# A unit's seventh product issued behind the first product of the next unit

## The chip, the cores and the metric

The kernel runs on one core of one Trainium2 chip, as one program with one launch. The metric is the device time of that program in microseconds (us). Five engines matter here: TensorE (PE, matrix products, with PEld for its weight loads), VectorE (DVE), ScalarE (ACT), GpSimd (POOL, which here issues accumulating transfers) and SyncE (SP, which issues the other transfers). Each engine runs its own instructions in a fixed order and waits on semaphores for the others.

## What is computed

The reference is a trunk of two layers over 528 rows (16 learned meta tokens and 512 tokens) of width 1024, in float32. Layer 0 mixes by retention, layer 1 by gated linear attention (GLA), and each layer has a half-step SwiGLU feed-forward part ahead of its mixer and one behind it:

```python
def swiglu(x, w_in, w_out):
    gate, up = jnp.split(x @ w_in, 2, axis=-1)      # 1024 -> 2 * 2816
    return (jax.nn.silu(gate) * up) @ w_out         # 2816 -> 1024

for i in range(DEPTH):                              # DEPTH = 2
    h = h + 0.5 * swiglu(rmsnorm(h, norm_ffn1[i]), ffn1_w_in[i], ffn1_w_out[i])
    hn = rmsnorm(h, norm_mix[i])
    h = h + (retention(hn, ...) if i % 2 == 0 else gla(hn, ...))
    h = h + 0.5 * swiglu(rmsnorm(h, norm_ffn2[i]), ffn2_w_in[i], ffn2_w_out[i])
return rmsnorm(h, final_norm)[:, N_META:]
```

Retention projects q, k, v and a gate g for four heads, rotates q and k, takes decayed scores in chunks, normalises per head, multiplies by silu(g) and projects back.

## The kernel before

**Precision.** Every float32 operand is held as two float32r parts, `hi` and `lo = x - hi`. One product of a 128-row block is therefore three matmuls (`mm3`, lines 473 to 475): hi by hi, hi weights by lo data, lo weights by hi data. A weight tile is split on arrival: ACT casts it to `whi` (line 167), DVE subtracts to get `wlo` (line 168).

**Units.** Most weight matrices are not multiplied tile by tile. Two output tiles of 128 rows, the two halves of the inner dimension and the two halves of the tokens make a 2 x 2 block product, which a *unit* does with seven products in place of eight (Winograd's form). `unit_steps` (line 667) issues them in the order `W.UNIT`: a11, s1, s2, a12, s3, s4, a22. Each is 12 matmuls of 264 columns in the feed-forward input and the retention, and 12 or 9 in the feed-forward output, by how many hidden tiles the group has (256 columns in the last feed-forward part). The letters a and s name the weights: a block of the matrix as it is, or a sum of blocks. s1 and s3 come from a `pair` tile, which SP loads (line 130) and POOL completes with an accumulating transfer (line 136); s2 and s4 are made by DVE in place (lines 173 and 175).

**Accumulators.** A unit has one PSUM bank X, out of a ring of four, and a tile QZ of two banks, out of two such tiles. The products a11, s2, s3 and a22 each need X, one after the other; s1, a12 and s4 go to QZ. So X has to be read out between any two of its products:

- after a11, ACT copies X away (line 695); then s2 may start, with s1 in between
- after s2, ACT copies X (line 699); then s3 may start, with a12 in between
- after s3, `c22` on DVE reads X (line 944 in a gate unit, 968 in an up unit, 1005 in an output unit); then a22 may start, with s4 in between
- after s4, `row1` reads QZ; after a22, `c21` reads X

**What is a unit where.** A feed-forward part (`ffn`, four of them: f10, f20, f11, f21) runs through groups of hidden tiles. For two hidden tiles at a time there is a gate unit g (`unit_g`, its `c21` is a Silu on ACT, line 948) and an up unit u (`unit_u`), after which `hidden` makes the seven combinations of the two hidden tiles and splits them (lines 642 to 644, and 506 and 507). Once a group is whole, its four output units o (`unit_o`) follow the next group's first g, ahead of that group's first u; the last group's follow its last u. Output units add to the residual `x`. In the retention, heads 1 to 3 have units for q, k, two for v and two for the gate; head 0 has units for its gate alone.

**What sets the order.** The code calls the steps in program order. A scheduler then lays the instructions out on each engine by priority; reads of accumulators are issued under `urgent()`, which puts them ahead. The weights follow a plan: `plan_ffn`, `plan_ret` and `plan_gla` list every product in the order of its use (`W.plan`), `get` takes the next entry and insists that it is the one asked for, and `fetch` (called by `hook` after each product) splits the entries ahead, into seven `whi`/`wlo` buffers. Raw loads (seven buffers) and pair loads (three) are begun as earlier ones are split.

Of the kernel before, what the change touches and what calls it, by code (L numbers as in the profile page):

```python
# [16 lines left out]
P = 128  # L17
# [52 lines left out]
class Weights:  # L70
# [10 lines left out]
    def __init__(self, tc, ctx, raw_bufs=7, pair_bufs=3, bufs=7):  # L81
        self.nc, self.tc = tc.nc, tc

        self.behind = None
        self.raw_pool = ctx.enter_context(tc.tile_pool(name="wraw", bufs=raw_bufs))
        self.pair_pool = ctx.enter_context(tc.tile_pool(name="wpair", bufs=pair_bufs))
        self.pool = ctx.enter_context(tc.tile_pool(name="wsplit", bufs=bufs))

        self.homes = [(self.pool, bufs, set())]
        self.ahead = AHEAD  # L90


        self.loads = {"raw": [], "pair": []}
        self.begun = dict.fromkeys(self.loads, 0)
        self.over = dict.fromkeys(self.loads, 0)
        self.room = {"raw": raw_bufs, "pair": pair_bufs}
        self.tiles, self.plan, self.parts = {}, [], {}
        self.split = self.taken = self.keys = 0

    def add(self, key, ap):  # L100
        c = self.keys
        self.keys += 1
        for o in range(0, ap.shape[1], PW):
            part = ap[:, o:o + PW]
            self.loads["raw"].append(((c, o), len(self.plan), (part,)))
            self.plan.append((key, c, o, part.shape[1], None))

    def add_unit(self, key, ap1, ap2, order, parted=False):
        c = self.keys
        self.keys += 1  # L110
        n = ap1.shape[1] // 2
        a = {"a11": ap1[:, :n], "a12": ap1[:, n:], "a21": ap2[:, :n], "a22": ap2[:, n:]}
        self.loads["pair"].append((c, len(self.plan), (a["a11"], a["a22"], a["a21"]), parted))
        for q in ("a11", "a12", "a22"):
            self.loads["raw"].append(((c, q), len(self.plan), (a[q],)))
        for q in order:
            self.plan.append((key + (q,), c, q, n, order))

# [70 lines left out]
    def get(self, key):  # L189

        i = self.taken
# [7 lines left out]
        return [(j,) + self.parts.pop(j) for j in range(i, i + n)]  # L199

# [39 lines left out]
def trunk(ctx, tc, a):  # L240
# [60 lines left out]
    def plan_ret():  # L301
        for h in range(RH):
            for j in (2 * h, 8 + 2 * h):
                if h:
                    W.add_unit(("rqk", j), a["ret_in"][j], a["ret_in"][j + 1], W.UNIT)
# [5 lines left out]
            for s, o in (("rv", 16), ("rg", 32)):  # L311
                for m in range(0, 4, 2):
# [4 lines left out]
                    else:  # L317
                        W.add_unit((s, h, m), a["ret_in"][c], a["ret_in"][c + 1], W.UNIT)
# [348 lines left out]
    def unit_steps(key, name, order, halves, ks, rhs, places, row1, c22, c21, behind=None):  # L667
# [8 lines left out]
        def step(q):  # L676
# [14 lines left out]
            with urgent():  # L691
# [12 lines left out]
                elif q == "a22":  # L704
                    c21(X)

# [8 lines left out]
    def unit(key, name, order, halves, ks, rhs, place, row1, c22, c21, behind=None):  # L715
# [40 lines left out]
    def ffn(which, layer, halves, gcol, u, feed, late=False):  # L756
# [7 lines left out]
        with tc.tile_pool(name=f"h_{me}", bufs=1) as hp, tc.tile_pool(name=f"t_{me}", bufs=1) as tp, \  # L764
# [189 lines left out]
            def unit_u(f, g, first):  # L954
# [16 lines left out]
                def c21(c):  # L971
                    V.scalar_tensor_tensor(y[0][:, 0], c, -1.0, g[1][:, a0:a1], ALU.mult, ALU.mult)
# [44 lines left out]
            for n, (kind, a_, b_) in enumerate(steps):  # L1017
# [39 lines left out]
                else:  # L1057
                    hs = [H[a_][f] for f in sorted(H[a_])]
# [3 lines left out]
                    break  # L1062

# [139 lines left out]
    def retention(u, feed):  # L1203
        with tc.tile_pool(name="retp", bufs=1) as rp, tc.tile_pool(name="wmore", bufs=2) as wp, psum_pool(4) as pp:
# [48 lines left out]
            def head(h):  # L1253
                qk = {}

                def rope_pair(s):
# [15 lines left out]
                    unit(("rqk", j), f"rqk{s}{h}", W.UNIT, HALVES, rows4_odd, rhs_u, place, row1, c22, c21)  # L1272
                    cos, sin = [tabs[s][:, c, :] for c in range(2)]
                    pa, pb = [tmp.tile([P, T], F32, tag="hf", name=f"r{i}{s}{h}") for i in "ab"]
                    V.tensor_mul(pa, t[0], cos)
                    V.tensor_mul(t[0], t[0], sin)
                    V.tensor_mul(pb, t[1], sin)
                    V.tensor_add(pa, pa, pb)
                    qk[s, 0], qk[s, 1] = [[rp.tile([P, T], F32R, tag=f"{s}{i}{m}", name=f"{s}{i}{m}_{h}")
                                           for i in range(2)] for m in range(2)]  # L1280
                    S.copy(qk[s, 0][0], pa)
                    V.tensor_mul(t[1], t[1], cos)
                    V.tensor_sub(t[0], t[0], t[1])
                    V.tensor_sub(qk[s, 0][1], pa, qk[s, 0][0].bitcast(F32))
                    split(qk[s, 1][0], qk[s, 1][1], t[0])
# [35 lines left out]
                def values():  # L1321
# [18 lines left out]
                    for m0 in (0, 2):  # L1340
# [11 lines left out]
                        unit(("rv", h, m0), f"rv{h}{m0}", W.UNIT, HALVES, rows4_odd, rhs_u, place, row1, c22, c21)  # L1352
# [64 lines left out]
                def gates(m0, use):  # L1417
# [19 lines left out]
                    unit(("rg", h, m0), f"rg{h}{m0}", W.UNIT, HALVES, rows4_odd, rhs_u, place, row1, c22, c21)  # L1437
# [785 lines left out]
```

## Time and profile before

| | |
|---|---|
| median of 3 runs | 2050.59 us (2050.23 to 2054.59) |
| profiled execution, its own time | 2055.57 us |
| its span, first to last instruction | 2053.8 us |
| PE busy in the span | 2026.1 us |
| DVE, ACT, POOL busy | 1794.8, 1198.9, 210.3 us |
| mean granted TensorE clock | 0.995 |

A profiled row has its start in us from the span's start, its duration, engine, line, operation, `out<-in` by the program's names without their numbers, and, in brackets, how long the engine stood idle before it and what ended that. A matmul is shown as about 0.28 us long while the next one starts 0.117 us later, since they are pipelined and their ends are modelled. So a gap between two matmuls shows as idle time only from about 0.16 us on, and the share of busy time hides shorter ones: where PE is looked at closely, starts are compared, not idle times.

### The profile page before, as it was taken

How to read it: one execution, taken by the hardware profiler on the slowest of the kernel's cores; microseconds unless marked ns; L12 is line 12 of the kernel's file. 1: busy time of each engine (PE TensorE's matmuls, PEld its weight loads, DVE VectorE, ACT ScalarE, POOL GpSimd, SP SyncE). 2: the span in 40 equal slices, each digit the busy share in tenths (PEclk: the TensorE clock that was granted, in tenths of full speed). 3: DMA queues.
4: the chain of work that ended last, by engine and by line, in shares of the span. 5: the costliest groups of instructions: out<-in, count | busy, mean ns of one | idle time of the engine just before them, and what ended most of it. 6: DMA issues, size and time to landing. Idle time of an engine off the chain costs nothing.

```text
span 2053.8 us, 43086 instructions
## 1 busy us (share of the span) xinstructions
PE 2026.1 (99%) x16335; PEld 1968.4 (96%) x16335; DVE 1794.8 (87%) x3299; ACT 1198.9 (58%) x2435; POOL 210.3 (10%) x181
## 2 busy tenths in 40 slices
PE   8999999999999999999999999999999999999998
PEld 8999999999999999999999999999899988999998
DVE  8988989968787889988898998989897968999996
ACT  5656666554545465656666665666645445666664
POOL 1011111000101000111111011111001000111110
PEclk9999999999999999999999999999999999999999
DMA  7676776445555532776876477676614351687762
GB/s 209 154 196 169 187 191 173 125 131 145 141 143 141 142 105 69 198 192 150 204 184 167 112 187 191 164 196 170 194 53 127 85 165 62 157 218 175 192 176 72
DMA packets 176112, 318.85 MB, mean 155 GB/s; under 512 B 17568, under 2 KB 40736, under 8 KB 175904
## 3 DMA queue, kind: packets, MB, share of 16 engines
q1 hardware_dynamic: 133856, 237.04, 34.8%
q0 software_dynamic: 40896, 75.51, 23.4%
q10 hardware_dynamic: 1152, 3.55, 0.6%
q8 instruction: 128, 2.10, 0.4%
q14 instruction: 80, 0.66, 0.1%
HBM read 311.76 MB, written 4.26 MB: 154 GB/s over the span
## 4 chain that ended last, share of the span: by engine, by line
PE 75%; DVE 16%; ACT 3%; issue 3%; DMA 2%; POOL 0%; SPq 0%; POOLq 0%; DVEq 0%; ACTq 0%
DVE wlo L168 5%; PE po_r L474 1%; PE po_r L475 1%; PE po_r L473 1%; ACT whi L167 1%; DVE hf L507 1%; PE Xf21o L473 1%; PE lv L1753 1%; PE Xf20o L473 1%; PE Xf20o L474 1%; PE Xf20o L475 1%; DVE unf L799 1%; PE Xf21o L475 1%; PE Xf21o L474 1%; PE Xf11u L473 1%
## 5 line engine op out<-in xcount | busy, mean ns | idle before, releaser
L167 ACT CAST whi<-raw 128x512 fp32r<-128x512 f32 (+1 forms) x893 | 525.3, 606 | 453.3 <-DVE raw L173 101.5
L168 DVE TENSOR_TENSOR wlo<-raw,whi 128x512 fp32r<-128x512 f32 (+1 forms) x893 | 586.0, 669 | 135.9 <-ACT whi L167 121.4
L167 ACT CAST whi<-pair 128x512 fp32r<-128x512 f32 (+1 forms) x304 | 183.9, 605 | 95.2 <-ACT su L695 12.8
L168 DVE TENSOR_TENSOR wlo<-pair,whi 128x512 fp32r<-128x512 f32 (+1 forms) x304 | 202.0, 664 | 5.5 <-ACT whi L167 5.4
L136 POOL DMA_DIRECT2D pair<-in_f_in x73 | 89.0, 1220 | 721.7 <-DVE wlo L168 247.8
L173 DVE TENSOR_TENSOR raw<-pair,raw 128x512 f32<-128x512 f32 (+1 forms) x146 | 97.3, 667 | 2.6
L175 DVE TENSOR_TENSOR raw<-raw,raw 128x512 f32<-128x512 f32 (+1 forms) x146 | 97.3, 666 | 2.5
L136 POOL DMA_DIRECT2D pair<-in_f_out x44 | 53.5, 1216 | 367.1 <-DVE wlo L168 118.0
L474 PE MATMUL po_r<-ogl,whi 128*128 128x264 f32 x256 | 71.3, 279 | 0.0
L473 PE MATMUL po_r<-ogh,whi 128*128 128x264 f32 x256 | 71.2, 278 | 0.0
L475 PE MATMUL po_r<-ogh,wlo 128*128 128x264 f32 x256 | 71.2, 278 | 0.0
L136 POOL DMA_DIRECT2D pair<-in_ret_in x20 | 24.4, 1222 | 298.7 <-DVE wlo L168 96.5
L473 PE MATMUL Xf20o<-hf,whi 128*128 128x264 f32 x176 | 50.3, 286 | 0.8 <-DVE x L1005 0.3
L473 PE MATMUL Xf10o<-hf,whi 128*128 128x264 f32 x176 | 50.3, 286 | 0.7 <-DVE x L1005 0.3
L473 PE MATMUL Xf11o<-hf,whi 128*128 128x264 f32 x176 | 50.2, 285 | 0.7 <-ACT hf L506 0.3
L474 PE MATMUL Xf10o<-hf,whi 128*128 128x264 f32 x176 | 49.2, 279 | 0.0
L474 PE MATMUL Xf20o<-hf,whi 128*128 128x264 f32 x176 | 49.1, 279 | 0.0
L474 PE MATMUL Xf11o<-hf,whi 128*128 128x264 f32 x176 | 49.1, 279 | 0.0
L475 PE MATMUL Xf10o<-hf,wlo 128*128 128x264 f32 x176 | 48.9, 279 | 0.0
L475 PE MATMUL Xf20o<-hf,wlo 128*128 128x264 f32 x176 | 48.9, 279 | 0.0
L475 PE MATMUL Xf11o<-hf,wlo 128*128 128x264 f32 x176 | 48.9, 279 | 0.0
L474 PEld LDWEIGHTS po_r<-ogl,whi 128*128 128x128 f32 x256 | 48.0, 188 | 0.0
(1172 smaller groups left out, 8520.1 us busy)
## 6 DMA issues: line engine op xcount, KB each, us to landing
raw<-in_f_in SPq DMA_DIRECT2D x277, 256.0 KB, 4.3
pair<-in_f_in SPq DMA_DIRECT2D x150, 256.0 KB, 4.4
pair<-in_f_in POOLq DMA_DIRECT2D x73, 512.0 KB, 6.9
raw<-in_f_out SPq DMA_DIRECT2D x80, 256.0 KB, 3.7
raw<-in_ret_in SPq DMA_DIRECT2D x76, 256.0 KB, 3.5
raw<-in_f_out SPq DMA_DIRECT2D x72, 192.0 KB, 3.2
pair<-in_f_out SPq DMA_DIRECT2D x48, 256.0 KB, 3.9
pair<-in_f_out POOLq DMA_DIRECT2D x24, 512.0 KB, 6.1
```

Source lines behind the costliest of these rows:

```text
L136: nc.gpsimd.dma_start(t, aps[2].unsqueeze(1).broadcast_to([P, 2, n]), accum_op=ALU.add)
L167: self.nc.scalar.copy(hi[:, :n], raw)
L168: V.tensor_sub(lo[:, :n], raw, hi[:, :n].bitcast(F32))
L173: V.tensor_add(s2, self.tiles[c][:, 1], self.tiles[c, "a11"])
L175: V.tensor_add(raw, raw, s2)
L473: nc.tensor.matmul(ps, lhsT=lh, rhs=rh, start=start, stop=False, **kw)
L474: nc.tensor.matmul(ps, lhsT=lh, rhs=rl, start=False, stop=False, **kw)
L475: return nc.tensor.matmul(ps, lhsT=ll, rhs=rh, start=False, stop=stop, **kw)
L507: V.tensor_sub(lo, src, hi.bitcast(F32))
L799: V.scalar_tensor_tensor(t[:, i, 1 - h, a0:], x[k][:, a0:], ngains[:, gcol + k:gcol + k + 1], rb[:, a0:], ALU.mult, ALU.mult)
L1753: nc.tensor.matmul(ps[:, j, J * P:J * P + n], lhsT=Kt[:, j, J * P:(J + 1) * P], rhs=q, start=(J == 0), stop=(J == 3), skip_group_check=True)
```

## The change

The last product of a unit, a22, is no longer issued as the unit's seventh. `unit` holds it back (`W.held`), the next unit issues its first product, and when that unit asks for its second, the plan has the held a22 first: `get` sees that the entry is not the one asked for and calls `settle`, which issues a22 with all that follows from it (`c21`, and what is now in `done`: `hidden` for an up unit, the rotation for q and k). The plan is written in the same order: `add_unit(..., hold=True)` takes a22 out and puts it behind the next unit's first product (`_planned`), or ahead of whatever else comes next in the plan. The order of loads, splits and frees follows the plan. Nothing else is computed, and no instruction is added or taken away.

Not held are: the up unit of the last two hidden tiles in the three feed-forward parts that are not the last one, the second v unit and the second gate unit of a retention head, and all GLA units. Where no unit follows (after a retention head's k, at the end of a feed-forward part) `settle` issues the held product where it stood before. Of the program's 150 units, 126 have their a22 behind the next one's first product: 27 gate units before an up unit, 9 gate units before an output unit, 35 up units before a gate unit, 36 output units before an output unit, 9 output units before an up unit, and 10 units in the retention.

```diff
@@ Weights
+        self.kept, self.held = [], None
...
     def add(self, key, ap):
+        self._planned()
...
+    def _planned(self):
+        self.plan += self.kept
+        self.kept = []
+
-    def add_unit(self, key, ap1, ap2, order, parted=False):
+    def add_unit(self, key, ap1, ap2, order, parted=False, hold=False):
...
         for q in order:
             self.plan.append((key + (q,), c, q, n, order))
+            self._planned()
+        if hold:
+            self.kept.append(self.plan.pop())
...
     def get(self, key):
+        if self.plan[self.taken][0] != key:
+            self.settle()
...
+    def settle(self):
+        held, self.held = self.held, None
+        if held:
+            held()
@@ plan_ffn, plan_ret
-                           last and b_ == LAST_GROUPS[1][0])
+                           last and b_ == LAST_GROUPS[1][0], last or (a_, b_) != ("u", NF - 2))
...
-                    W.add_unit(key, w_out[layer, b_, :, c], w_out[layer, b_ + 1, :, c], W.UNIT, last and a_ == 0)
+                    W.add_unit(key, w_out[layer, b_, :, c], w_out[layer, b_ + 1, :, c], W.UNIT, last and a_ == 0, True)
...
-                    W.add_unit(("rqk", j), a["ret_in"][j], a["ret_in"][j + 1], W.UNIT)
+                    W.add_unit(("rqk", j), a["ret_in"][j], a["ret_in"][j + 1], W.UNIT, hold=True)
...
-                        W.add_unit((s, h, m), a["ret_in"][c], a["ret_in"][c + 1], W.UNIT)
+                        W.add_unit((s, h, m), a["ret_in"][c], a["ret_in"][c + 1], W.UNIT, hold=m == 0)
@@ unit_steps, unit
                 elif q == "a22":
                     c21(X)
+            if q == "a22" and done:
+                done()
...
-        for st in unit_steps(key, name, order, halves, ks, rhs, places, row1, c22, c21, behind):
+        *steps, last = unit_steps(key, name, order, halves, ks, rhs, places, row1, c22, c21, behind, done)
+        for st in steps:
             st()
+        if hold:
+            W.held = last
+        else:
+            last()
@@ ffn, unit_u
+                def done():
+                    if f < NPL:
+                        todo.append((f, y[0]))
+                    elif not last:
+                        hidden(f, y[0])
+
                 unit((which, layer, "i", "u", f), f"{me}u{f}", W.FIRST if first else W.UNIT, halves, rows4, rhs_in,
-                     place_of[0], row1, c22, c21)
-                if f < NPL:
-                    todo.append((f, y[0]))
-                elif not last:
-                    hidden(f, y[0])
+                     place_of[0], row1, c22, c21, None, done, not last)
...
+            W.settle()
```

Three places show what moves. The first is PE where up unit 18 of the first feed-forward part (f10) follows gate unit 18: the first and last matmul of each product from the gate unit's s4 on, before and now (`Xf10g18` is the gate unit's bank X, `Xf10u18` the up unit's, `QZ` the two-bank tiles).

```order
L475 MATMUL QZf10g18_3844<-uhf10_153,wlo175_3880 128x264
L473 MATMUL Xf10g18_3843<-thf10_231,whi176_3898 128x264
...
L475 MATMUL Xf10g18_3843<-thf10_231,wlo176_3899 128x264
L473 MATMUL Xf10u18_3978<-uhf10_153,whi177_3917 128x264
...
L475 MATMUL Xf10u18_3978<-uhf10_153,wlo177_3918 128x264
L473 MATMUL QZf10u18_3979<-thf10_231,whi178_3934 128x264
...
L475 MATMUL QZf10u18_3979<-thf10_231,wlo178_3935 128x264
L473 MATMUL Xf10u18_3978<-thf10_231,whi179_3952 128x264
```

And in the changed program:

```order
L494 MATMUL QZf10g18_3812<-uhf10_153,wlo175_3880 128x264
L492 MATMUL Xf10u18_3958<-uhf10_153,whi176_3898 128x264
...
L494 MATMUL Xf10u18_3958<-uhf10_153,wlo176_3899 128x264
L492 MATMUL Xf10g18_3811<-thf10_231,whi177_3916 128x264
...
L494 MATMUL Xf10g18_3811<-thf10_231,wlo177_3917 128x264
L492 MATMUL QZf10u18_3959<-thf10_231,whi178_3934 128x264
...
L494 MATMUL QZf10u18_3959<-thf10_231,wlo178_3935 128x264
L492 MATMUL Xf10u18_3958<-thf10_231,whi179_3952 128x264
```

The gate unit's a22 and the up unit's a11 have changed places. Between s3 and a22 of the gate unit now stand two products (s4 and the other unit's a11) where there was one, and between a11 and s2 of the up unit also two (the other unit's a22 and s1).

The second place is ACT over the same stretch: the gate unit's Silu steps (`gf`), the copies out of the up unit's X and QZ, and the weight casts among them. Before:

```order
L940 ACTIVATE gf1018_3841<-gf1018_3841 128x528
L948 ACTIVATE gf1019_3842<-Xf10g18_3843 128x264
L167 CAST whi182_4014<-raw86_3690 128x512
L167 CAST whi183_4033<-raw87_3733 128x512
L167 CAST whi184_4052<-raw88_3752 128x512
L695 COPY su3_3980<-Xf10u18_3978 128x264
L167 CAST whi185_4069<-pair34_3712 128x512
L693 COPY su3_3980<-QZf10u18_3979 128x264
L167 CAST whi186_4088<-raw88_3752 128x512
L699 COPY su3_3980<-Xf10u18_3978 128x264
```

Now:

```order
L966 ACTIVATE gf1018_3809<-gf1018_3809 128x528
L714 COPY su3_3960<-Xf10u18_3958 128x264
L178 CAST whi182_4014<-raw86_3693 128x512
L178 CAST whi183_4033<-raw88_3770 128x512
L178 CAST whi184_4051<-raw87_3733 128x512
L974 ACTIVATE gf1019_3810<-Xf10g18_3811 128x264
L178 CAST whi185_4069<-pair34_3712 128x512
L712 COPY su3_3960<-QZf10u18_3959 128x264
L178 CAST whi186_4088<-raw88_3770 128x512
L718 COPY su3_3960<-Xf10u18_3958 128x264
```

The copy that frees the up unit's X after a11 (L695, now L714) has moved ahead of three weight casts, and the gate unit's `c21` (L948, now L974) behind them.

The third place is ACT after that up unit, where gate unit 20 begins: the casts of `hidden` (`hf1018`) and the copies out of the gate unit's X and QZ. Before:

```order
L506 CAST hf1018_4114<-su3_4073 128x3x264
L695 COPY su3_4130<-Xf10g20_4128 128x264
L506 CAST hf1018_4114<-t0f10h18_4115 128x2x264
L167 CAST whi191_4202<-raw91_3902 128x512
L693 COPY su3_4130<-QZf10g20_4129 128x264
L167 CAST whi192_4219<-pair35_3862 128x512
L506 CAST hf1018_4114<-t1f10h18_4116 128x2x264
L699 COPY su3_4130<-Xf10g20_4128 128x264
```

Now:

```order
L714 COPY su3_4098<-Xf10g20_4096 128x264
L178 CAST whi191_4201<-raw90_3883 128x512
L525 CAST hf1018_4140<-t0f10h18_4141 128x2x264
L525 CAST hf1018_4140<-su3_4073 128x3x264
L712 COPY su3_4098<-QZf10g20_4097 128x264
L178 CAST whi192_4219<-pair35_3850 128x512
L525 CAST hf1018_4140<-t1f10h18_4142 128x2x264
L718 COPY su3_4098<-Xf10g20_4096 128x264
```

The copy after a11 is now ahead of all casts of `hidden`; the copy after s2 (L699, now L718) still stands behind the last of them, and these now belong to a product that PE does one product later than before.

More of the change, by code (lines that the diff above doesn't have):

```diff
@@ L665, in trunk, with unit_steps @@
     ends = {}
-    def unit_steps(key, name, order, halves, ks, rhs, places, row1, c22, c21, behind=None):
+    def unit_steps(key, name, order, halves, ks, rhs, places, row1, c22, c21, behind=None, done=None):
         started, hold = set(), {}
@@ L713, in rows4_odd, with unit @@
         return range(4) if what[0] == "n" and what != "n3" else ODD
-    def unit(key, name, order, halves, ks, rhs, place, row1, c22, c21, behind=None):
+    def unit(key, name, order, halves, ks, rhs, place, row1, c22, c21, behind=None, done=None, hold=True):
         wd = width(halves)
@@ L1350, in c21 @@
                             S.copy(vt[m0 + 1][:, a0:a1], c)
[L1352 removed]
+                        unit(("rv", h, m0), f"rv{h}{m0}", W.UNIT, HALVES, rows4_odd, rhs_u, place, row1, c22, c21,
+                             hold=m0 == 0)
                 def turn(j):
@@ L1435, in c21 @@
                         use(m0 + 1, a0, a1, o)
-                    unit(("rg", h, m0), f"rg{h}{m0}", W.UNIT, HALVES, rows4_odd, rhs_u, place, row1, c22, c21)
+                    unit(("rg", h, m0), f"rg{h}{m0}", W.UNIT, HALVES, rows4_odd, rhs_u, place, row1, c22, c21, hold=m0 == 0)
                     sgs.extend(mine)
```

30 lines of the change are left out of this document (16 added, 14 removed).

## The prediction

> **What bounds the kernel.** The page comes first: busy shares and the chain that ended last.
>
> ```profile
> PE 2026.1 (99%) x16335; PEld 1968.4 (96%) x16335; DVE 1794.8 (87%) x3299; ACT 1198.9 (58%) x2435; POOL 210.3 (10%) x181
> PE 75%; DVE 16%; ACT 3%; issue 3%; DMA 2%; POOL 0%; SPq 0%; POOLq 0%; DVEq 0%; ACTq 0%
> ```
>
> PE is the bound: busy for 99%, and three quarters of the chain. Its idle time, 2053.8 - 2026.1 = 27.7 us, looks like all that a new order could win, and most of it lies outside the units. But a matmul counts as busy for 0.28 us while the next starts 0.117 us later, so short gaps are hidden in the 99%. I therefore measure stretches against the pitch: the view of busy time by stretches, cut at the starts of units. The columns are the stretch, its length, then busy time and instructions of PE, PEld, DVE, ACT and POOL, the granted clock, DMA share and GB/s.
>
> ```profile
> 61.93:113.12 51.19, 50.56 (x422) 49.78 (x421) 50.23 (x89) 34.38 (x70) 6.10 (x5) 1.00 0.71 175
> 113.12:152.32 39.20, 39.20 (x338) 39.20 (x337) 34.31 (x58) 21.77 (x43) 4.87 (x4) 1.00 0.74 192
> 152.32:212.61 60.29, 60.08 (x506) 59.34 (x505) 53.36 (x95) 37.51 (x77) 7.30 (x6) 1.00 0.67 162
> 212.61:243.62 31.01, 31.01 (x255) 30.54 (x254) 27.68 (x55) 19.03 (x42) 4.04 (x4) 1.00 0.77 202
> 243.62:314.19 70.57, 70.23 (x590) 69.25 (x589) 62.27 (x108) 43.73 (x89) 9.35 (x8) 1.00 0.77 194
> 314.19:355.90 41.71, 40.98 (x338) 40.08 (x337) 40.85 (x79) 28.66 (x61) 3.65 (x3) 1.00 0.62 155
> 819.18:1112.61 293.43, 291.65 (x2438) 288.05 (x2437) 266.40 (x475) 183.45 (x376) 35.30 (x29) 1.00 0.72 182
> 1163.22:1456.48 293.26, 291.51 (x2437) 287.64 (x2436) 266.03 (x471) 183.10 (x373) 36.36 (x30) 1.00 0.74 186
> 1812.93:1871.48 58.55, 58.49 (x507) 57.70 (x505) 54.80 (x98) 37.45 (x77) 8.46 (x7) 1.00 0.78 187
> 1871.48:1901.77 30.29, 30.29 (x254) 29.52 (x253) 27.27 (x55) 18.88 (x42) 3.61 (x3) 1.00 0.77 207
> ```
>
> The second row is four output units without any wait: 9.80 us for the 84 matmuls of each (a row's count takes in two or so that overlap its edges), 1.40 us for a product of 12. The first six rows are the first feed-forward part. It has 5 g and u units (49.0 us without waits, 51.19 taken), these 4 o units, 6 g and u (58.8, 60.29), 4 o with 9 matmuls in a product (29.4, 31.01), 7 g and u (68.6, 70.57), 4 o (39.2, 41.71). The excess is 2.2 + 0 + 1.5 + 1.6 + 2.0 + 2.5 = 9.8 us. The second and third parts hold the same 30 units from their second one on (284.2 us): 9.2 and 9.1 us of excess. In the last part a product of 12 should take 1.36 us (256 columns in place of 264, and the pitch in proportion); six g and u units would need 57.1 (58.55 taken), four o units 28.6 (30.29), and three such rounds give about 9. Together **37 us of waits inside units**, though PE shows up as full.
>
> **What the change takes away.** Where do they lie? I go through a gate unit and its up unit by starts: the stretch of each, then the gate unit's a22 on PE and DVE.
>
> ```profile
> 273.71:283.73 10.02, 10.02 (x87) 9.90 (x86) 9.93 (x18) 6.51 (x13) 1.22 (x1) 1.00 0.73 179
> 283.73:293.98 10.25, 10.15 (x87) 9.95 (x86) 8.12 (x15) 6.33 (x13) 1.21 (x1) 1.00 0.75 188
> 281.99 0.28 PE L475 MATMUL QZf10g<-uhf,wlo 128*128 128x264 f32 x1
> 282.19 0.39 PE L473 MATMUL Xf10g<-thf,whi 128*128 128x264 f32 x1
> 282.42 0.28 PE L474 MATMUL Xf10g<-tlf,whi 128*128 128x264 f32 x1
> 281.71 0.42 DVE L944 TENSOR_TENSOR gf<-Xf10g,su 128x264 f32<-128x264 f32 x1
> ```
>
> a22 starts 0.20 us behind the last matmul of s4, not 0.117, and 0.06 us after `c22` on DVE (281.71 + 0.42 = 282.13) has read X; its second matmul comes 0.23 us later, not 0.117. That is 0.08 + 0.11 us, and the unit's whole excess is 10.02 - 9.80 = 0.22 us. In the new order the up unit's a11 stands ahead of it: 1.40 us where some 0.1 lacked, so the wait goes. Next the up unit's s2, on PE and ACT:
>
> ```profile
> 286.41 0.28 PE L475 MATMUL QZf10u<-thf,wlo 128*128 128x264 f32 x1
> 286.79 0.39 PE L473 MATMUL Xf10u<-thf,whi 128*128 128x264 f32 x1
> 283.98 0.65 ACT L940 ACTIVATE gf<-gf 128x528 f32<-128x528 f32 x1 [1.39 <-DVE gf L939]
> 284.81 1.65 ACT L167 CAST whi<-raw 128x512 fp32r<-128x512 f32 x3
> 286.36 0.38 ACT L695 COPY su<-Xf10u 128x264 f32<-128x264 f32 x1
> ```
>
> s2 starts 0.38 us behind the matmul ahead of it, just after the copy of a11 ends (286.74). That copy stood behind three weight casts on ACT, and these behind the Silu that waited for DVE. The unit loses 10.25 - 9.80 = 0.45 us, most of it here (0.26 us, and a refill as behind a22). Now a22 and s1 both stand between a11 and s2, 1.40 us more, and the copy is ahead of the casts: gone. Then an output unit with 9 matmuls in a product:
>
> ```profile
> 218.70 0.43 DVE L1005 SCALAR_TENSOR_TENSOR x<-Xf10o,x 128x264 f32<-128x264 f32 x1
> 218.97 0.28 PE L475 MATMUL QZf10o<-hf,wlo 128*128 128x264 f32 x1
> 219.18 0.39 PE L473 MATMUL Xf10o<-hf,whi 128*128 128x264 f32 x1
> 219.40 0.29 PE L474 MATMUL Xf10o<-hf,whi 128*128 128x264 f32 x1
> ```
>
> The same: a22 follows the end of `c22` (219.13), and 0.10 + 0.10 us are lost, some 0.22 with the refill. One product more is 1.05 us: gone.
>
> For the first part: 9 gate units by 0.22 (2.0 us), 6 of the 9 up units by 0.45 (2.7; the stretches of g and u have 5.7 us of excess, so the gate units leave 3.7, room for 8 at most), 4 o units by 0.22 (0.9), and about 0.5 in the last group, most of whose 2.5 us is the wait for `hidden` of the unit that isn't held. That is 6.1 of 9.8 us, 62%; what stays is mainly s3's wait for the copy of s2, and that `hidden`. I take 64% of 37 for all four parts: 24 us. The retention adds little:
>
> ```profile
> L473 PE MATMUL Xrqkq<-rth,whi 128*128 128x264 f32 x36 | 10.6, 295 | 0.1
> L473 PE MATMUL Xrg<-rth,whi 128*128 128x264 f32 x96 | 27.1, 283 | 0.2 <-ACT su L695 0.2
> ```
>
> A matmul that starts a product after a wait is shown longer than 0.278 us (0.39 above), so the mean of its group tells the sum: for q and the gate (17 x 36 + 5 x 96) ns = 1.1 us, and 0.3 idle. Taken away in all: **25 us**.
>
> **What it moves, and may cost.** No instruction is added, so the moved ones are what to price. The third place in the section on the change is the tight one: the copy that frees a gate unit's X after s2.
>
> ```profile
> 293.15 0.70 DVE L960 TENSOR_TENSOR su<-su,QZf10u 128x528 f32<-128x528 f32 x1
> 294.99 0.42 DVE L972 SCALAR_TENSOR_TENSOR su<-Xf10u,gf 128x264 f32<-128x264 f32 x1
> 298.33 0.64 ACT L506 CAST hf<-t1f10h 128x528 fp32r<-128x528 f32 x1
> 298.86 0.39 ACT L699 COPY su<-Xf10g 128x264 f32<-128x264 f32 x1
> 299.55 0.28 PE L473 MATMUL Xf10g<-thf,whi 128*128 128x264 f32 x1
> ```
>
> Today the copy ends at 299.25 and s3 starts at 299.55, unhindered: 0.3 us to spare. Now I lay the new order on from E, the end of the up unit's s4, with these durations: E = 293.98 - 1.40 = 292.58. DVE reaches `c21` at E + 3.6 (there is 2.4 before, and two more steps of 0.6 now stand ahead of it; a22 itself ends at E + 2.8, plus the 0.2 by which a matmul's end is shown later), and the three steps behind it that finish `t1` end at E + 5.5. ACT, with the copy of s1 and a weight cast up to E + 5.9, casts `t1` up to E + 6.4 and copies X up to E + 6.8; s3 would start at E + 7.0. So 0.2 us are left: I take 0, with the wait at s2 today (0.45 us) as the upper end, at 35 places 16 us. On the other side nothing can be won there, since s3 has no wait.
>
> The weights are wanted one product earlier (a11) and given back one later (a22):
>
> ```profile
> pair<-in_f_in POOLq DMA_DIRECT2D x73, 512.0 KB, 6.9
> 234.49 1.21 POOL L136 DMA_DIRECT2D pair<-in_f_in  x1 [8.05 <-DVE raw L175]
> 246.57 0.69 DVE L173 TENSOR_TENSOR raw<-pair,raw 128x512 f32<-128x512 f32 x1
> ```
>
> Nearly the shortest case: 12.1 us from issue to first use, 6.9 to land. Two products (2.1 to 2.8 us) less still leave over 2 us, so 0. If that cover went, one late pair would cost about a product. DVE keeps its work in a stretch that gets some 1% shorter: 54.80 of 58.55 us, 94%, becomes 95%, still not full. At the ends of three feed-forward parts the residual steps of the last units come one product later beside the statistics; with q's rotation on DVE I put 3 us on all of these together (six to nine places, one DVE step of 0.4 to 0.7 us each), between 0 and 6.
>
> Sum: 25 - 3 = **22 us**. The profiled execution (2055.57, of which 2053.8 is span) would come to 2033.6; it lies 5.0 above the median of 2050.59, and from the median it is **2028.6 us**.
>
> **The clock.** The granted clock falls to half now and then: its mean, and the longest drop with the stretch ahead of it.
>
> ```profile
> core 0: 2053.8 us, clock 0.995
> 408.00:412.00 4.00, 2.38 (x20) 1.00 0.63 98
> 412.20:419.10 6.90, 6.81 (x35) 0.51 0.08 16
> ```
>
> (The columns are length, PE busy, clock, DMA share and GB/s.) PE was busy for 2.38 of 4.00 us, and then ran 6.9 us at half speed: 3.4 us lost, and (1 - 0.995) x 2053.8 = 10 in all. If the drops fall otherwise once the time has shifted, some of this is won or as much lost again: I leave the sum as it is and let the range move by 4 us, one such drop. [...]
>
> **The rivals.**
> - *The wait moves on to s3.* If the copy after s2 comes 0.2 to 0.5 us later than laid out, s3 of a gate unit waits as s2 does today: 35 x 0.45 = 16 of the 25 us come back: 2041.6. For it: 0.2 us of margin, and DVE 0.4 us behind at L960 (293.15, though s4 ended at 292.58 + 0.2). Against it: the copy follows `t1` by one cast alone.
> - *Slower.* The same place, but decided by DVE: if `c21` of the up unit stands 1.2 us later than E + 3.6, behind weight steps, each of the 35 gate units waits 1.0 us and loses 35, against 25 won: 2060. From 0.9 us on (0.2 spare, then 35 x 0.7 = 25) it is a loss. Against it: the new order puts just two more steps (0.6 us each) ahead of `c21`, and these are counted.
> - *No change.* Waits return in the same amount elsewhere (weights, a full DVE): 2050. Against it: DVE at 95%, pairs with 2 us over.
> - *The clock.* The drops vanish, but for the one at the start (-8), or as many more come (+8): 2021 or 2037.
>
> **How the numbers follow.** Forecast 0.66 (2022 to 2034), s3 0.17, clock 0.05, no change 0.06, slower 0.06. A measurement of this kernel can tell some 0.2% (4 us) from no change. Faster: 0.66 + 0.17 + 0.05 = 0.88; same 0.06; slower 0.06. The range runs from the forecast with all waits gone, nothing returned and a better clock (2050.6 - 25 - 4, some 2021, taken down to 2020) to the s3 rival (2042), which leaves out some 0.15.
>
> **What would show it.** Right: a pair of g and u units takes 19.6 to 19.7 us, not 10.02 + 10.25; a four-unit stretch of 9-matmul o units takes 30.1, not 31.0; DVE keeps its busy time. Wrong: s3 of a gate unit starts late behind L718, PE waits for `wlo`, or DVE waits for a pair transfer.

## The result and the profile after

| | before | after |
|---|---|---|
| median, run side by side | 2052.01 us (4 runs, 2050.23 to 2054.59) | 2030.13 us (4 runs, 2029.49 to 2031.01) |
| profiled execution, its own time | 2055.57 | 2029.62 |
| its span | 2053.8 | 2027.9 |

The ratio is 0.9893, with a 95% interval from 0.9881 to 0.9906: some 22 us less, against 2028.6 us forecast.

First the page of the changed kernel, busy shares and the chain that ended last:

```profile
PE 2005.1 (99%) x16335; PEld 1957.0 (97%) x16335; DVE 1787.5 (88%) x3299; ACT 1207.2 (60%) x2435; POOL 209.0 (10%) x181
PE 78%; DVE 15%; issue 2%; ACT 2%; DMA 2%; POOL 0%; SPq 0%; POOLq 0%; DVEq 0%; ACTq 0%
```

Nothing is to be seen there: PE stands at 99% as before, since the short waits were hidden in that share. So again the stretches, cut where the first product of the same units starts as in the prediction (columns as there). The pair of gate unit 18 and up unit 18 stands behind the six stretches of the first feed-forward part; then come the second and the third part and two stretches of the last.

```profile
61.28:111.14 49.86, 49.07 (x411) 48.18 (x409) 49.59 (x88) 34.40 (x69) 6.10 (x5) 1.00 0.66 165
111.14:150.34 39.20, 39.20 (x339) 39.20 (x337) 33.53 (x58) 21.63 (x43) 4.87 (x4) 1.00 0.78 201
150.34:209.31 58.97, 58.97 (x506) 58.93 (x505) 53.08 (x94) 37.94 (x76) 7.30 (x6) 1.00 0.71 171
209.31:239.80 30.49, 30.49 (x258) 30.43 (x256) 27.85 (x56) 19.20 (x43) 3.65 (x3) 1.00 0.76 194
239.80:309.65 69.85, 69.85 (x599) 69.85 (x598) 63.13 (x110) 44.90 (x89) 9.74 (x8) 1.00 0.77 195
309.65:351.07 41.42, 41.08 (x338) 39.90 (x337) 41.37 (x80) 29.29 (x62) 4.86 (x4) 1.00 0.71 178
268.92:288.54 19.62, 19.62 (x171) 19.62 (x169) 17.93 (x32) 13.03 (x26) 2.90 (x3) 1.00 0.73 190
809.02:1099.02 290.00, 289.35 (x2451) 287.72 (x2450) 267.01 (x477) 186.83 (x378) 37.78 (x31) 1.00 0.74 186
1145.36:1435.39 290.03, 289.30 (x2451) 287.65 (x2450) 267.13 (x474) 186.04 (x375) 36.54 (x30) 1.00 0.75 190
1788.15:1846.73 58.58, 58.58 (x504) 58.51 (x502) 53.21 (x96) 37.79 (x76) 8.46 (x7) 1.00 0.75 184
1846.73:1876.84 30.11, 30.11 (x257) 30.05 (x256) 27.40 (x56) 19.01 (x43) 3.61 (x3) 1.00 0.81 212
```

A stretch now holds the a22 of the unit ahead of it and not that of its own last unit, so some are longer or shorter by a product. With that allowed for, the first part's excess over its pitch is 2.3, 0, 0.2, 0.7, 0.2 and 2.2 us: 5.6, where it was 9.8. (First row: five units less a product, 47.6 us; fourth: three matmuls more than 29.4 us, 29.75; fifth: a 9-matmul product more than 68.6 us, 69.65.) The pair takes 19.62 us instead of 20.27. The second and third parts have one a22 more in the stretch (1.40 us), so they compare as 288.60 with 293.43 and 288.63 with 293.26: **4.8 and 4.6 us less**, an excess of 4.4 where 9.2 and 9.1 were.

Two things in these rows were not forecast. The first group (first row) has gained nothing, and the last part next to nothing (last two rows). In the first groups stands a wait that was short or absent before, at a12. PE and ACT of the changed kernel in the third part:

```profile
1180.28 0.28 PE L494 MATMUL Xf11u<-thf,wlo 128*128 128x264 f32 x1
1180.80 0.39 PE L492 MATMUL QZf11u<-uhf,whi 128*128 128x264 f32 x1 [0.24 <-ACT su L712]
1177.93 0.64 ACT L525 CAST hf<-t1f11h 128x528 fp32r<-128x528 f32 x1 [0.40 <-DVE t1f11h L663]
1178.53 0.62 ACT L178 CAST whi<-raw 128x512 fp32r<-128x512 f32 x1
1179.06 0.38 ACT L974 ACTIVATE gf<-Xf11g 128x264 f32<-128x264 f32 x1
1179.34 1.13 ACT L178 CAST whi<-raw 128x512 fp32r<-128x512 f32 x2
1180.37 0.38 ACT L712 COPY su<-QZf11u 128x264 f32<-128x264 f32 x1
```

a12 writes one bank of the tile QZ and waits until ACT has copied s1 out of the other (1180.37 + 0.38 = 1180.75). That copy stands behind the held gate unit's Silu (L974), which has moved to this place, and three weight casts. There is one product between s1 and a12, 1.40 us. In the kernel before, the same unit looked like this:

```profile
1195.43 0.28 PE L475 MATMUL QZf11u<-thf,wlo 128*128 128x264 f32 x1
1195.84 0.39 PE L473 MATMUL Xf11u<-thf,whi 128*128 128x264 f32 x1
1196.74 0.39 ACT L693 COPY su<-QZf11u 128x264 f32<-128x264 f32 x1
1197.35 0.28 PE L473 MATMUL QZf11u<-uhf,whi 128*128 128x264 f32 x1
```

Here s2 waits: it starts 0.41 us behind the last matmul of s1 and not 0.117. The copy of s1 ends at 1197.13, and a12 starts 0.22 us later without a wait. Without the 0.29 us that s2 had waited, and with ACT as it is, a12 would have come before the end of that copy: part of the wait at a12 was hidden behind the one at s2. Summed over all units by starts against the pitch, waits at a12 rose from some 4.4 to 9.2 us, while those at a22 fell from 17.1 to 2.3 and those at s2 from 11.9 to 1.8. In this stretch PE goes on with s2 into X while ACT copies s1 out of QZ (1196.74 to 1197.13), and its matmuls still start 0.11 to 0.12 us apart. That a12 waits because the program keeps one order for the whole tile, though its two banks are in use by one engine each, is the author's estimate: no run here tried a12 without the wait.

### The profile page after: what moved, and what is told of

Same layout as the page of the kernel before. It is cut to its first block, busy times and chain, and to the rows that moved or that the text cites. A ratio compares the mean times of both kernels' runs of the same rounds, so it can differ in the third digit from the quotient of the medians.

```text
span 2027.9 us, 43043 instructions
## 1 busy us (share of the span) xinstructions
PE 2005.1 (99%) x16335; PEld 1957.0 (97%) x16335; DVE 1787.5 (88%) x3299; ACT 1207.2 (60%) x2435; POOL 209.0 (10%) x181
## 4 chain that ended last, share of the span: by engine, by line
PE 78%; DVE 15%; issue 2%; ACT 2%; DMA 2%; POOL 0%; SPq 0%; POOLq 0%; DVEq 0%; ACTq 0%
DVE wlo L179 5%; PE po_r L493 1%; PE po_r L492 1%; PE po_r L494 1%; DVE hf L526 1%; PE Xf11o L492 1%; PE Xf11o L493 1%; PE Xf11o L494 1%; PE lv L1786 1%; DVE unf L825 1%; PE Xf21o L492 1%; PE Xf21o L493 1%; PE Xf21o L494 1%; PE QZf11o L492 1%; PE Xf20u L492 1%
```

## The experiments

**Which units matter.** Three versions of the changed kernel hold a22 in some kinds of unit only. `g_only`: gate units. `o_only`: output units. `no_u`: all but up units. The edit for `g_only`; the others set the same flags otherwise, and the plan of the weights has them too:

```diff
@@ unit_u, unit_o
-                     place_of[0], row1, c22, c21, None, done, not last)
+                     place_of[0], row1, c22, c21, None, done, False)
...
-                unit((which, layer, "o", gi, d), f"{me}o{gi}{d}", W.UNIT, halves, ks, rhs, place_of[0], row1, c22, c21, behind)
+                unit((which, layer, "o", gi, d), f"{me}o{gi}{d}", W.UNIT, halves, ks, rhs, place_of[0], row1, c22, c21, behind, hold=False)
```

> The changed kernel, but in the feed-forward parts only gate units hold their a22 (up and output units do theirs seventh, as before); the retention as changed. Theory (what is won is the hand-over of X: the gate units' a22 behind c22, 8 us in all, and the up units' s2 behind the copy of a11, 7.3 us): 15 us are won there, some 1.5 come back at the up units' a12, which now waits for the copy of s1, and the retention gives 2: 2036 to 2038 us; output units keep a22 waits of about 6 us. Rival (the gain comes from the other order of the weights, or from clock drops that fell otherwise, and goes with the number of held products, 36 of the 116 in these parts): about 2045.

> The changed kernel, but in the feed-forward parts only output units hold their a22; the retention as changed. Theory: their own a22 waits (6 us) go, some 1 of it comes back at a12, and the retention gives 2: 2045 us, with gate and up units waiting as before (10.0 and 10.25 us long). Rival (gain by the number of held products, 45 of 116): about 2043, so the time alone doesn't tell the two apart here; the waits in the trace do.

> The changed kernel, but up units of the feed-forward parts do their a22 seventh; gate and output units hold theirs. The up units' a22 had hardly a wait before (0.6 us in three parts), while the gate unit behind a held one waits at a12 for the copy of s1 (1.6, 0.7 and 0.6 us in three parts). Theory (hand-over of X): holding them wins nothing and costs 2 to 3 us, so 2026 to 2030 us. Rival (by the number of held products, 35 of 116): 6 us lost, 2036.

Measured, beside 2051.72 us of before (7 runs): 2038.56 us (ratio 0.9935, interval 0.9918 to 0.9952), 2041.96 (0.9949, 0.9930 to 0.9967) and 2029.73 (0.9891, 0.9876 to 0.9907). The second feed-forward part in each, in that order; with up units not held, it compares with 293.43 and 288.60 as it stands:

```profile
813.80:1103.89 290.09, 289.16 (x2439) 286.90 (x2438) 265.76 (x475) 184.58 (x376) 35.31 (x29) 1.00 0.73 184
...
820.65:1113.01 292.36, 290.93 (x2438) 287.37 (x2437) 266.48 (x476) 184.21 (x378) 36.53 (x30) 1.00 0.73 184
...
811.07:1099.50 288.43, 287.88 (x2439) 286.08 (x2438) 265.75 (x476) 185.49 (x378) 37.07 (x31) 1.00 0.74 187
```

Gate units give 3.3 of the 4.8 us, output units 1.1, up units nothing. The gain goes with the waits that were there and not with the number of held products (36, 45 and 35): the rival is out. By their times `g_only` lies 0.6 us above its theory's range and `no_u` at the upper end of its own: that holding the up units costs 2 to 3 us was not borne out. The 3 us that `o_only` won beyond its expectation are about what the entry of the GLA gives (below), which it has as well.

**The hand-over of X by itself.** If a22 waits because X must be read out first, then a bank of its own should free it with no change of order. `b_a22` gives a22 of each unit in the feed-forward parts and the retention a second bank out of the ring, in the kernel before; `b_s2` gives one to s2, s3 and a22 together; `b_both` has three banks, for a11, for s2 and s3, and for a22. All three leave out the sums across the banks. The edit for `b_a22`:

```diff
+            own = into == "X" and q in ('a22',) and name[0] in "fr"
+            if own and "own" not in hold:
+                hold["own"] = bank("Y" + name)[:, :X.shape[-1]]
+            if own:
+                X = hold["own"]
```

> The kernel before with its order kept, but a22 of a unit (feed-forward parts and retention) goes to a bank of its own out of the same ring, so that it need not wait until c22 has read X; it leaves out the sum with the products before it in X. Theory (a22 starts late because X has to be read out first): its waits, 15 to 16 us in the trace of before outside the GLA, go without any change of order: 2036 to 2038 us; the up units' s2 keep theirs. Rival (a22 starts late for its weights or its data): about 2051, as before.

> The kernel before with its order kept, but s2, s3 and a22 of a unit go to a bank of their own, and only a11 to X, so that s2 need not wait for the copy of a11; it leaves out the sum of a11 with the products behind it. Theory: the waits at s2 (11 us outside the GLA) go, and those at a22 stay: 2040 to 2042 us. Rival (s2 waits for its weights, or the copies on ACT hold up the next product in its place): about 2051.

> The kernel before in its old order, with three banks for a unit: a11 in X, s2 and s3 in a second, a22 in a third; it leaves out the sums across these. A bank for a22 alone had won 3 us and one for s2 alone 1 us, and what went at one of the two came back for the most part at the next hand-over. Theory (there are two hand-overs in a row, behind a11 and behind s3, and whichever is relieved alone lets PE run into the other, so that only both together pay): 2027 to 2033 us, as the changed kernel, with a22 and s2 both near 2 us. Rival (PE is held by ACT and DVE whatever the order, and the wait goes on to a12 and s3): 2043 to 2048.

Measured: 2048.00 us (ratio 0.9990, 0.9978 to 1.0001) and 2049.54 (0.9998, 0.9989 to 1.0007), both beside 2050.81 (25 runs), and `b_both` 2040.73 beside 2050.32 (0.9956, 0.9942 to 0.9969). The first two expectations were far off, and the third lies between its theories. Gate unit 18 and up unit 18 of the second part show why. The kernel before, then `b_a22`, `b_s2` and `b_both`:

```profile
1030.46:1040.51 10.05, 10.05 (x86) 9.92 (x85) 9.96 (x18) 6.51 (x13) 1.21 (x1) 1.00 0.67 184
1040.51:1050.70 10.19, 10.12 (x87) 9.91 (x85) 8.07 (x15) 6.36 (x13) 1.22 (x1) 1.00 0.86 211
```

```profile
1027.76:1037.56 9.80, 9.80 (x86) 9.80 (x85) 9.71 (x18) 6.51 (x13) 1.21 (x1) 1.00 0.75 194
1037.56:1047.95 10.39, 10.07 (x87) 9.87 (x85) 8.32 (x15) 6.31 (x13) 1.22 (x1) 1.00 0.87 216
```

```profile
1028.50:1038.52 10.02, 10.02 (x86) 9.90 (x85) 9.93 (x18) 6.51 (x13) 1.21 (x1) 1.00 0.69 174
1038.52:1048.32 9.80, 9.80 (x86) 9.80 (x85) 8.08 (x15) 6.34 (x13) 1.22 (x1) 1.00 0.85 212
```

```profile
1023.77:1033.57 9.80, 9.80 (x87) 9.80 (x85) 9.71 (x18) 6.52 (x13) 1.21 (x1) 1.00 0.77 179
1033.57:1043.37 9.80, 9.80 (x87) 9.80 (x85) 8.13 (x15) 6.32 (x13) 1.22 (x1) 1.00 0.84 212
```

The bank does free a22 (9.80 us, no wait). But the up unit behind it then takes 10.39 instead of 10.19: the copy of a11 that s2 waits for ends when ACT gets to it, so PE only arrives 0.2 us earlier at the same end. With a bank for s2 its wait goes and that at a22 stays (10.02 and 9.80). With both, the pair takes the 19.60 us of the changed order. The whole second part, in the same three kernels, beside 293.43 of before:

```profile
817.44:1109.48 292.04, 289.52 (x2439) 286.72 (x2438) 266.10 (x475) 183.27 (x376) 35.31 (x29) 1.00 0.73 183
...
817.80:1109.74 291.94, 290.57 (x2439) 287.28 (x2438) 267.07 (x475) 183.16 (x376) 36.41 (x30) 1.00 0.74 184
...
814.65:1104.19 289.54, 288.58 (x2439) 286.56 (x2438) 266.61 (x476) 183.13 (x376) 36.55 (x30) 1.00 0.73 185
```

So `b_both` gains 3.9 of the 4.8 us with no product moved. The stretch begins with the part's second unit; counted from the part's first matmul on, the part takes 341.1 us before, 336.2 in `b_both` and 336.3 in the changed kernel, so there it gains all of it. The hand-over of X is the cause of the gain in these parts. Relieved alone, a22 gives 1.4 us: most of its wait is paid again at s2. s2 alone gives 1.5 (2.3 from the first matmul on), so it isn't true that only both together pay.

The times of `b_s2` and `b_both` hide this, since they lose elsewhere or gain nothing there. Against the second profile of before (below), `b_both` is 0.5 us longer in the retention and 0.9 in the GLA's stage, and its entry of the third part is as long as before; the changed kernel is shorter in all three, by 1.9, 2.7 and 1.8 us. So what the changed kernel gains at the two entries does not come from freeing X. In the retention of `b_both` PE does a12 of each of the three q units right behind s1, ahead of s2, and waits for the copy of s1, 2.2 us in all. At a12 it waits 12 us in the whole program, more than the changed kernel, though no Silu has moved: copies that ACT does no earlier hold up a PE that comes earlier.

**Two products instead of one, and each kind at its best.** `second` issues the held a22 behind the next unit's second product. `mixed` does that for gate units, keeps output units as in the changed kernel and doesn't hold up units.

```diff
@@ add_unit, second
             self.plan.append((key + (q,), c, q, n, order))
-            self._planned()
+            if q != order[0]:
+                self._planned()
@@ add_unit, mixed
-            self._planned()
+            if q != order[0] or not self.far:
+                self._planned()
+        self.far = far
```

> The changed kernel, with the held a22 behind the next unit's second product in place of its first (a11, s1, held a22, s2, ...). Then two products stand between s1 and a12 where there is one now, and still two between a11 and s2. Theory (the 9 us at a12 are waits for the copy of s1, which ACT does behind the held unit's Silu and weight casts): most of the 6 us of these that the change added go, 2024 to 2027 us; and if the slow stretch of the last part (117.6 ns between two matmuls of 256 columns in place of 113.3, entered each time at an a12 that waited) stays out with them, 3 to 5 us more, 2020 to 2023. Rival (a12 waits for its weights, which follow the plan): the same 2030. Second rival (c21 and what follows, one product later again, holds up s3 of the next unit, 35 x 0.45 us): 2040 and more.

> The changed kernel with each kind of unit in the feed-forward parts where its waits were least: a gate unit's a22 behind the next unit's second product, an output unit's behind the first, an up unit's seventh as before. Theory (waits add up by place: the up units' a12 waits, 1.9 us over the four parts, go, and nothing comes back, since the gate unit behind an up unit that isn't held has its casts of hidden early): 2027 to 2029 us. Rival (as in the runs so far, what goes at one hand-over comes back at the next): 2030.

Measured: 2030.23 us (0.9893, 0.9876 to 0.9910) and 2030.08 (0.9910, 0.9895 to 0.9925), no better than the changed kernel and above what both theories had. In `second` a12's waits fell as forecast, from 9.2 to 3.3 us, and those at s3 rose from 3.3 to 12.6. From its waits in the second part (waited for: us in total, times, longest):

```profile
PE Xf20g L493 <- ACT su L719: 0.5, 1, 0.5
PE Xf20o L493 <- DVE x L1034: 0.4, 1, 0.4
PE Xf20o L493 <- ACT hf L526: 0.3, 1, 0.3
PE Xf20o L493 <- ACT szf L719: 0.2, 1, 0.2
```

L719 is the copy after s2, which frees X for s3: the wait has moved on by one product. In `mixed` the second part is the shortest of all, 288.2 us, but 0.4 us a part is less than chance does in the last one (below).

**The margin at s3.** `dup_s2` is the changed kernel with the copy after s2 done twice.

```diff
                 elif q == "s2":
-                    S.copy(s_[:, 1] if first else ab[:, 1], X)
+                    for _ in range(2):
+                        S.copy(s_[:, 1] if first else ab[:, 1], X)
```

> The changed kernel with the copy that frees X after s2 done twice on ACT (0.38 us more, the same values). In the changed kernel s3 of a gate unit starts 0.23 to 0.28 us behind the end of that copy, against 0.05 where it has to wait for it. Theory (the margin of about 0.2 us is real, and every gate unit is that near to the s3 wait): 27 gate units lose some 0.18 us and 0.11 for the refill, about half of the up and output units as much, 15 to 19 us in all: 2045 to 2049 us. Rival (ACT has room, and the copy's place doesn't matter): 2030 to 2033.

Measured: 2049.51 us (ratio to before 1.0001, 0.9991 to 1.0010). 0.38 us more on ACT, which is busy for 60%, take back the whole gain, 19 us; waits at s3 rise from 3.3 to some 33 us, while those at a12 fall by 5. The order on PE isn't quite the same: in 34 units the scheduler put the first matmuls of s4 ahead of s3. Every gate unit of the feed-forward parts now waits at s3, so the place was as near to the edge as it looked, but all but a few up units and nearly all output units do as well, and the output units have the largest share, 12 us: the small margin was not special to the gate units.

**The retention.** `ret_off` is the changed kernel with the retention's units not held (`hold=False` at its four calls).

> The changed kernel with the retention's units as before (a22 seventh), the feed-forward parts as changed. By the prediction's term (1.1 us at a22 and 0.3 of idle time): 1.4 us more, 2031 to 2032 us, and in the trace the retention's a22, s2 and a11 waits are back. Rival (the retention gave 2 to 3 us, since heads 1 to 3 got shorter by so much in the changed kernel's trace): 2032.5 to 2033.

Measured: 2032.35 us (2029.22 to 2040.24), too wide to tell 1 us. By the trace, the stretch from the end of the first feed-forward part to the start of the second takes 411.9 us in it and 411.6 in the changed kernel: 0.3 us, from one profile each. The waits at the retention's s2 and a22 are back, by some 1.5 us, but not those at a11.

**The same kernels again.** Both kernels were profiled a second time, unedited.

> The changed kernel, nothing edited, profiled a second time. Theory (which of the two pitches the last part's matmuls have, 113.3 or 117.6 ns, is settled by chance at each wait): the slow stretches lie elsewhere than at 1803 to 1875 and 1891 to 1941 us, and their number differs from 100 of 195 products. Rival (it follows from the order of the program): the same stretches again.

> The kernel before, nothing edited, profiled a second time. Theory (the clock drops at 412, 1118 and 1463 us and the two pitches of the last part are settled by chance): some of these drops are missing or there are others, and the slow pitch lies elsewhere. Rival: the same drops and stretches, and then the 3 to 4 us that the changed kernel saved there are an effect of its order.

Their times were 2032.58 and 2054.62 us (one run each). The second and third part repeat to 0.3 us; first the kernel before, then the changed one (less 1.40 us, 288.51 and 288.58):

```profile
818.64:1112.02 293.38, 291.59 (x2439) 288.02 (x2437) 266.30 (x475) 183.36 (x376) 35.31 (x29) 1.00 0.73 182
1161.47:1454.99 293.52, 291.76 (x2439) 287.97 (x2438) 266.14 (x471) 183.01 (x373) 35.91 (x30) 1.00 0.74 186
```

```profile
811.27:1101.18 289.91, 289.27 (x2451) 287.60 (x2450) 266.92 (x477) 186.85 (x378) 37.72 (x31) 1.00 0.73 186
1147.57:1437.55 289.98, 289.23 (x2451) 287.59 (x2449) 267.00 (x474) 186.03 (x375) 36.54 (x30) 1.00 0.74 190
```

What doesn't repeat are the clock drops and the pitch of the last part. Apart from the last microseconds, half clock (granted 0.50 or 0.51 for 3.4 to 6.9 us at a time, in the first profile of before) stood at 50, 412, 1119 and 1463 us of the kernel before, and at 8, 49, 411 and 1462 the second time; at 8 alone in the changed kernel, and at 8 and 408. The theory on the pitch holds (its slow stretches are counted in the last section). That on the drops holds in part: the one at 1119 was missing the second time, and those at 412 and 1463 came again. The one at 1463 stands behind a wait of PE (1.2 us, shown below). All five profiles with the old order have this wait, 1.2 to 1.6 us long, and four of them, all but that of `b_a22`, a drop behind it; neither profile of the changed kernel has it, nor any of the other seven that hold products.

## Why the prediction was right, step by step

The median fell by 21.9 us where 22 was forecast, but parts of the sum were off both ways. These are the differences between the two second profiles (spans 2052.8 and 2030.8), by the starts of the first and last matmul of each part:

| part | forecast | measured |
|---|---|---|
| waits in the units of the first three feed-forward parts | -18 | 4.0 + 4.8 + 4.8: -13.6 |
| the same in the last part | -6 | -1.8 |
| entry of the third part and of the GLA | a share of +3 | -1.8 and -2.7 |
| the retention stage, entry included | -1.4 | -1.9 |

- **The waits that go** were right in place and size. In the first three parts a22 and s2 stood for 19.1 us of excess before and 2.2 after, 16.9 us, where 64% of the excess there came to 18. The pair takes 19.62 us (forecast 19.6 to 19.7). The four output units take 30.49; without the three matmuls more of a gate unit's a22 that is 30.14 (forecast 30.1).
- **"Waits return nowhere" failed**, at a12 and not at s3. In the same parts a12 rose from 2.2 to 6.4 us and s3 by 0.7. I had followed the copy that frees X through ACT's row, and not the copy of s1 two places ahead of it, though the order shows it: in an up unit the held gate unit's Silu stands in front of it. That is about a third of the wait, 2.1 us in five units; gate units (1.7 us) and output units (2.2 us) wait there without it. Which step holds those wasn't traced; `b_both` waits at such places too, with no product moved.
- **The s3 rival** had its margin right. A gate unit in the changed kernel:

```profile
294.93 0.38 ACT L718 COPY su<-Xf10g 128x264 f32<-128x264 f32 x1
295.46 0.28 PE L494 MATMUL QZf10g<-uhf,wlo 128*128 128x264 f32 x1
295.58 0.28 PE L492 MATMUL Xf10g<-thf,whi 128*128 128x264 f32 x1
```

  s3 starts 0.12 us behind the matmul ahead of it, so without waiting, and 0.27 us behind the end of the copy (295.31). Where it has to wait it starts 0.05 behind, so 0.2 us are spare, as laid out. `dup_s2` shows what the rival would have cost: 19 us where 16 were laid out. The rival's time was added up without a term: 2041.6 is 25 less 16 off the median and leaves out the 3 us of the ends; with them it is 2044.6, above the range.
- **The last part was sized wrongly.** 64% of 9 us was taken over from the others. But part of its excess was no wait: its matmuls have two pitches (below), and the slower one cost 3.3 us of the excess before and 5.7 after in the first profiles, 6.1 and 6.3 in the second ones.
- **The ends had the wrong sign.** At the entry of the third part and of the GLA, before, PE waits (the view of waits, between 1111 and 1122 us and between 1455 and 1475), and ACT stands at a weight cast whose load lands late; the normalising of the last rows is queued behind that cast:

```profile
PE pf11g L473 <- ACT uhf L553: 0.8, 1, 0.8
PE st_n L599 <- DVE sqa_n L570: 1.2, 1, 1.2
1114.98 0.62 ACT L167 CAST whi<-raw 128x512 fp32r<-128x512 f32 x1 [0.30 <-DMA raw<-in_f_in]
1457.38 0.62 ACT L167 CAST whi<-raw 128x512 fp32r<-128x512 f32 x1 [2.35 <-DMA raw<-in_gla_in]
```

  In the changed kernel neither wait is left, and the GLA's cast waits less:

```profile
1434.45 0.62 ACT L178 CAST whi<-raw 128x512 fp32r<-128x512 f32 x1 [0.69 <-DMA raw<-in_gla_in]
```

  In the GLA's case the clock drop that followed the wait (0.51 for 3.4 us) went with it. That the cast waits less for its load is shown; which step of the plan brings it isn't, since `g_only` and `o_only` have the shorter entry of the GLA too. The kernels with more banks, whose plan is that of before, don't have it.
- **The retention** gave 0.3 us by its held products, not 1.4; the rest of the stage's 1.9 isn't traced to a cause.
- **Weights, pairs and DVE** cost nothing, as forecast: in the second and third part PE waits for no `wlo`, and DVE's busy time is 1787.5 us beside 1794.8.

So the mechanism, and its size in the first three parts, hold where they were read from rows. That is 13.6 of the 22 us. The 4.5 us at the two entries came from elsewhere, as `b_both` shows, and most of the retention's 1.9 is not explained. 4 us came back at a12, 4 us in the last part weren't there to be won, and the ends, guessed as a cost, made good for them: that the sum met the time to 2 us is partly luck.

## What to carry to other kernels

When several products take turns in one accumulator, measure all hand-overs of the round before pricing one: a wait that is relieved alone can be paid at the next (`b_a22`: 0.25 us at a gate unit, 0.20 back in the up unit behind it), and relieving it can uncover the next tight one (a12 behind s2: waits of 2.2 us before and 6.4 us after in the first three parts). Read what an experiment gives by stages, since its time can hide a gain that another stage takes back (`b_s2`). When an instruction is moved, go through each engine's new order and ask of every accumulator read behind the moved step how much time it has left, not only of the one that looks tightest. Where PE is shown 99% busy, compare starts with the pitch, and check the pitch itself in each stage.

## What the runs showed of the hardware

**Two pitches.** In the last feed-forward part, whose matmuls have 256 columns, the time between starts is either 113.3 or 117.6 ns, for tens of microseconds on end. Three stretches of the same profile of the changed kernel, without a wait and at full clock, the first two of 84 matmuls and the third of 81:

```profile
1807.16:1817.05 9.89, 9.89 (x87) 9.89 (x85) 8.06 (x14) 5.96 (x13) 1.22 (x1) 1.00 0.74 193
1974.31:1983.83 9.52, 9.52 (x86) 9.52 (x85) 9.09 (x17) 6.27 (x13) 0.00 (x0) 1.00 0.31 83
1788.15:1797.33 9.18, 9.18 (x83) 9.18 (x82) 7.66 (x14) 5.17 (x10) 1.22 (x1) 1.00 0.93 252
```

That is 117.7, 113.3 and 113.3 ns. In the profiles of before and of the changed kernel, some two thirds of the changes from the one to the other stand at a product that had waited or right behind one. Of 195 groups of 12 matmuls, 56 and 107 were slow in the two profiles of before, and 100 and 113 in those of the changed kernel, at other places; among all kernels with one bank X it was between 34 (`second`) and 135 (`mixed`), which is 1.8 to 7.0 us. With 264 columns no such long slow stretch was seen: the pitch was 116.7 ns, but in about one product in seven, many of them behind a wait, several starts in a row were 120 to 129 ns apart. At the a12 of a gate unit of the changed kernel (86.3 us) the starts behind the wait came after 226, 129, 122, 123, 129, 121 and 123 ns, and then at the pitch. The cause of the two pitches isn't known; the DMA traffic alone doesn't decide it, since the fast pitch stands beside 83 and 252 GB/s, and the slow one beside 193.
